# A two-layer decoder trunk: the copies of the latent keys and values out of PSUM move from VectorE to ScalarE

## The chip, the core and the metric

The kernel runs on one core of a Trainium2 chip. The metric is the device time of one execution in microseconds (us), given as a median over runs. Besides it there is one profiled execution of the kernel, from which every row below is taken.

## The reference: what is computed

The model has two layers over 256 tokens of width 1024. In each layer one wide input projection feeds three causal attentions side by side: a block-sparse one (A, 8 heads), a latent one (B, 8 heads) and a differential one (C, 4 heads). Each is gated and projected back, the three results are merged by sigmoid gates, projected once more, and a gated embedding and a layer norm end the layer. The change lies in the latent attention, of which this is the core:

```python
cq = _rmsnorm(b_cq, gq)                  # 256 x 384
ckv = _rmsnorm(b_ckv, gkv)               # 256 x 256
qh = _split_heads(cq @ w_uq, MLA_HEADS)
q_b = concat([qh[..., :64], rope(qh[..., 64:])])
kvh = _split_heads(ckv @ w_ukv, MLA_HEADS)
k_b = concat([kvh[..., :64], broadcast(rope(b_kr))])   # keys: 64 + 32 per head
yb = mla_attention(q_b, k_b, kvh[..., 64:])            # values: 64 per head
```

The product `ckv @ w_ukv` gives the latent keys (64 of the 96 rows of every head's key) and the latent values.

## The kernel before, in words

**Precision and weights.** Every large product is made of three matmuls: each operand is split into a high part (rounded to the fast 32-bit format) and a low part (the rest), and high x high, high x low and low x high are summed in PSUM (`mm3`, lines 236 to 239). Each piece of the weights is loaded on SP's queue into one of five raw buffers (line 167), cast to its high part on ScalarE (line 173) and subtracted to its low part on VectorE (line 174). There are three buffers for split pieces, so a cast can wait for TensorE to be done with an older piece; a raw buffer is free for the next load when the subtraction has read it.

**PSUM.** The eight banks form two pools of four. `ps_w` serves the projections in rotation: a projection takes the bank that the fourth one before it used, and has to wait until that one has been copied out. `ps_t` serves transposes, scores and attention outputs.

**Order of the work.** TensorE's order is written by hand: a list of projections ("fill") with the attention steps put in by due times (lines 923 to 984). The order of the other engines comes from a scheduler, engine by engine, each executing its queue in order. Around the change TensorE runs, in each layer: a gate projection (`gate`, bank name `pg`), transposes of attention A's probabilities (`tr_p`, bank name `tp`), the latent keys in two groups of four heads (`up_kn`, bank name `pn`), the latent values for two blocks of 128 tokens (`up_v`, bank name `pk`), again transposes, then the next gate projection (weights `hi_m`, `lo_m`), more of attention A, and the gate path of attention B (weights `hi_bz`, `lo_bz`, bank name `pa`). The four banks before that gate projection are thus the two `pn` and the two `pk`, and the gate projection takes over the bank of the first `pn`.

**Copies out of PSUM.** `nope` (lines 583 to 596) is used for the latent queries (tile `qb`) and keys (tile `kb`). Its bank holds 128 rows, two heads of 64 rows on top of each other; the upper half (`e == 0`) is copied by ScalarE (line 594), the lower half by VectorE (line 596). `up_v` copies its whole bank on VectorE (line 630) into tile `vb`. Keys are used by the scores of attention B (`sc`, lines 678 and 681), values some 50 us later (line 737).

Of the kernel before, what the change touches and what calls it, by code (L numbers as in the profile page):

```python
# [31 lines left out]
def tile_decoder_trunk(  # L32
# [24 lines left out]
    nc = tc.nc  # L57
# [25 lines left out]
    def bank(pool, name):  # L83
        return pool.tile([P, 512], F32, tag="bank", name=name)
# [143 lines left out]
    def W(key):  # L228
        i = state["use"]
        assert pieces[i][0] == key, (pieces[i][0], key)  # L230
        split_to(i + 1 + SPLIT_AHEAD)
        load_to(i + 1 + SPLIT_AHEAD + LOAD_AHEAD)
        state["use"] += 1
        return parts.pop(i)

    def mm3(o, lh, ll, rh, rl, start, stop):
        nc.tensor.matmul(o, lh, rh, start=start, stop=False)  # L237
        nc.tensor.matmul(o, lh, rl, start=False, stop=False)  # L238
        nc.tensor.matmul(o, ll, rh, start=False, stop=stop)  # L239
# [34 lines left out]
    NQ, NK = 3, 2  # L274
# [62 lines left out]
    def layer(li):  # L337
# [14 lines left out]
        T = {}  # L352
# [227 lines left out]
            nc.gpsimd.tensor_tensor(dst[:, :, 16:32], ta[:, :nh, 16:32], tb[:, :nh, 0:16],  # L580
                                    op=ALU.add)

        def nope(dst, w, act_t, nk, g2):
            o = bank(ps_w, "pn")
            for j in range(2):
                c0 = (2 * g2 + j) * P
                for k in range(nk):
                    mm3(o[:, j * S:(j + 1) * S], w[0][:, k, c0:c0 + P], w[1][:, k, c0:c0 + P],
                        act_t[:, 0, k, :], act_t[:, 1, k, :], k == 0, k == nk - 1)
            d = dst[0:64, 4 * g2:4 * g2 + 4, :].rearrange("p (j e) t -> p j e t", e=2)  # L590
            for e in range(2):
                src = o[64 * e:64 * e + 64, :].rearrange("p (j t) -> p j t", j=2)
                if e == 0:
                    nc.scalar.copy(d[:, :, e, :], src)
                else:
                    nc.vector.tensor_copy(d[:, :, e, :], src)  # L596

        def up_qn(g2):
            if g2 == 0:
                T["uqN"] = W(K("uqN"))  # L600
                T["qb"] = work.tile([P, 8, S], F32, tag="qk8", name=f"qb{li}")[:96]
            nope(T["qb"], T["uqN"], yc4, NQ, g2)
# [13 lines left out]
        def up_kn(g2):  # L616
            if g2 == 0:
                T["ukv"] = W(K("ukv"))
                T["kb"] = work.tile([P, 8, S], F32, tag="qk8", name=f"kb{li}")[:96]
            nope(T["kb"], [t[:, 0] for t in T["ukv"]], T["ckvT"], NK, g2)  # L620

        def up_v(b):
            if b == 0:
                T["vb"] = work.tile([P, 2, 512], F32, tag="v", name=f"vb{li}")
            wh, wl = [t[:, 1] for t in T["ukv"]]
            o = bank(ps_w, "pk")
            for k in range(NK):
                mm3(o, T["ckvT"][:, 0, k, b * P:(b + 1) * P], T["ckvT"][:, 1, k, b * P:(b + 1) * P],
                    wh[:, k, :], wl[:, k, :], k == 0, k == NK - 1)
            nc.vector.tensor_copy(T["vb"][:, b, :], o)  # L630

        def rope_k():
            for b in range(2):
# [297 lines left out]
        fill += [(2.13, up_qn, (0,)), (2.13, up_qn, (1,)), (1.06, up_qr, (0,)), (1.06, up_qr, (1,))]  # L931
        g_a(1)
        fill += [(1.42, up_kn, (0,)), (1.42, up_kn, (1,)), (1.4, up_v, (0,)), (1.4, up_v, (1,))]
        g_a(2)
        fill += [(H, bz, (g, j)) for g in range(2) for j in range(2)]
# [253 lines left out]
```

## Time and profile before

| | |
|---|---|
| median of 3 runs | 655.67 us (655.61 to 655.78) |
| the profiled execution, its own time | 656.14 us |
| its span in the trace | 654.4 us |
| ScalarE (ACT) busy | 368.5 us (56%), 729 instructions |
| GpSimd (POOL) busy | 109.8 us (17%) |
| granted TensorE clock, mean | 0.997 |

The span runs from the first to the last instruction of the trace; the execution's own time holds 1.7 us around it. Engines are PE (TensorE matmuls), PEld (its weight loads), DVE (VectorE), ACT (ScalarE), POOL (GpSimd) and SP (the DMA queue). Times in rows are microseconds from the span's start; L596 is line 596 of the kernel. A matmul's busy time reaches to its modelled end, so neighbours overlap: in a stream without waits a 256-column matmul starts every 0.12 us though each is shown with 0.28 us.

### The profile page before, as it was taken

How to read it: one execution, taken by the hardware profiler on the slowest of the kernel's cores; microseconds unless marked ns; L12 is line 12 of the kernel's file. 1: busy time of each engine (PE TensorE's matmuls, PEld its weight loads, DVE VectorE, ACT ScalarE, POOL GpSimd, SP SyncE). 2: the span in 40 equal slices, each digit the busy share in tenths (PEclk: the TensorE clock that was granted, in tenths of full speed). 3: DMA queues.
4: the chain of work that ended last, by engine and by line, in shares of the span. 5: the costliest groups of instructions: out<-in, count | busy, mean ns of one | idle time of the engine just before them, and what ended most of it. 6: DMA issues, size and time to landing. Idle time of an engine off the chain costs nothing.

```text
span 654.4 us, 11980 instructions
## 1 busy us (share of the span) xinstructions
PE 638.8 (98%) x4623; PEld 595.2 (91%) x4623; DVE 464.2 (71%) x884; ACT 368.5 (56%) x729; POOL 109.8 (17%) x139
## 2 busy tenths in 40 slices
PE   9999998999999999999999999989999999999994
PEld 6999988999989999988879999989998899999884
DVE  5658798786787566655895587987867866566566
ACT  5457685555675545544455576755656655444451
POOL 2060452010003220000020605511100032200002
PEclk9999999999999999999999999999999999999998
DMA  8765177454546665665446652774445465766511
GB/s 284 239 223 154 58 238 245 124 158 133 158 145 210 195 186 171 191 194 187 127 117 192 196 158 74 230 247 124 138 130 173 149 198 159 204 182 185 169 33 64
DMA packets 82796, 110.31 MB, mean 169 GB/s; under 512 B 3962, under 2 KB 59700, under 8 KB 82740
## 3 DMA queue, kind: packets, MB, share of 16 engines
q1 hardware_dynamic: 80832, 106.25, 53.0%
q10 hardware_dynamic: 1908, 3.31, 1.6%
q8 instruction: 36, 0.59, 0.4%
q14 instruction: 20, 0.16, 0.1%
HBM read 108.49 MB, written 1.05 MB: 167 GB/s over the span
## 4 chain that ended last, share of the span: by engine, by line
PE 66%; issue 15%; DVE 10%; ACT 5%; DMA 2%; POOL 2%; POOLq 0%; DVEq 0%; ACTq 0%
PE pg L237 5%; PE pg L239 5%; PE pg L238 5%; PE pa L237 5%; PE pa L238 5%; PE pa L239 5%; PE pb L239 5%; PE pb L238 5%; PE pb L237 4%; PE pbr L237 3%; PE pbr L239 3%; PE pbr L238 3%; PE sc L681 2%; PE pv L737 2%; PE tp L724 1%
## 5 line engine op out<-in xcount | busy, mean ns | idle before, releaser
L237 PE MATMUL pg<-act,hi_m 128*128 128x256 f32 x384 | 109.5, 285 | 4.6 <-DVE kb L596 3.4
L239 PE MATMUL pg<-act,lo_m 128*128 128x256 f32 x384 | 107.9, 281 | 0.0
L238 PE MATMUL pg<-act,hi_m 128*128 128x256 f32 x384 | 107.9, 281 | 0.0
L174 DVE TENSOR_TENSOR lo_m<-raw_m,hi_m 128x1024 fp32r<-128x1024 f32 x48 | 59.4, 1241 | 25.5 <-ACT hi_m L173 25.5
L237 PEld LDWEIGHTS pg<-act,hi_m 128*128 128x128 f32 x384 | 72.4, 188 | 5.3 <-DVE kb L596 3.9
L173 ACT CAST hi_m<-raw_m 128x1024 fp32r<-128x1024 f32 x48 | 49.7, 1053 | 43.4 <-PE pg L238 29.0
L238 PEld LDWEIGHTS pg<-act,hi_m 128*128 128x128 f32 x384 | 72.4, 189 | 0.1
L239 PEld LDWEIGHTS pg<-act,lo_m 128*128 128x128 f32 x384 | 72.4, 188 | 0.0
L237 PE MATMUL pbr<-act,hi_b 128*128 128x256 f32 x128 | 37.4, 292 | 0.0
L239 PE MATMUL pbr<-act,lo_b 128*128 128x256 f32 x128 | 36.0, 281 | 0.0
L238 PE MATMUL pbr<-act,hi_b 128*128 128x256 f32 x128 | 35.9, 281 | 0.0
L174 DVE TENSOR_TENSOR lo_b<-raw_b,hi_b 128x1024 fp32r<-128x1024 f32 x24 | 32.8, 1379 | 1.2 <-ACT hi_b L173 1.2
L173 ACT CAST hi_b<-raw_b 128x1024 fp32r<-128x1024 f32 x24 | 24.6, 1050 | 14.8 <-PE pbr L238 6.1
L1057 POOL TENSOR_TENSOR bnmv<-bnmv,mhalf 128x1 f32<-128x1 f32 x4 | 3.1, 780 | 164.4 <-DVE bnmv L1056 164.4
L174 DVE TENSOR_TENSOR lo_wo<-raw_wo,hi_wo 128x1024 fp32r<-128x1024 f32 x16 | 19.3, 1223 | 15.7 <-ACT hi_wo L173 15.7
L907 POOL TENSOR_TENSOR gz<-gz,subt 128x512 f32<-128x512 f32 x4 | 9.2, 2310 | 111.3 <-DVE sm1('c', 3)_6089 L695 53.7
L174 DVE TENSOR_TENSOR lo_pg<-raw_pg,hi_pg 128x1024 fp32r<-128x1024 f32 x16 | 19.2, 1221 | 9.4 <-ACT hi_pg L173 9.4
L173 ACT CAST hi_pg<-raw_pg 128x1024 fp32r<-128x1024 f32 x16 | 16.4, 1049 | 16.6 <-issue 7.2
L237 PE MATMUL pb<-hi_wo,act 128*128 128x512 f32 x64 | 25.5, 398 | 0.0
L238 PE MATMUL pb<-lo_wo,act 128*128 128x512 f32 x64 | 25.3, 395 | 0.0
L239 PE MATMUL pb<-hi_wo,act 128*128 128x512 f32 x64 | 25.3, 395 | 0.0
L173 ACT CAST hi_wo<-raw_wo 128x1024 fp32r<-128x1024 f32 x16 | 16.3, 1048 | 15.1 <-issue 12.1
(900 smaller groups left out, 2209.8 us busy)
## 6 DMA issues: line engine op xcount, KB each, us to landing
raw_m<-in_w_merge_dram SPq DMA_DIRECT2D x48, 512.0 KB, 3.7
raw_wo<-in_w_out_dram SPq DMA_DIRECT2D x16, 512.0 KB, 4.6
raw_pg<-in_w_ple_gate_dram SPq DMA_DIRECT2D x16, 512.0 KB, 4.4
raw_aq<-in_w_in_dram SPq DMA_DIRECT2D x8, 512.0 KB, 4.6
raw_ak<-in_w_in_dram SPq DMA_DIRECT2D x8, 512.0 KB, 5.5
raw_az<-in_w_in_dram SPq DMA_DIRECT2D x8, 512.0 KB, 5.8
raw_bz<-in_w_in_dram SPq DMA_DIRECT2D x8, 512.0 KB, 4.9
raw_b<-in_w_branch_a_dram SPq DMA_DIRECT2D x8, 512.0 KB, 4.7
```

Of the source, the lines that this page charges most:

```text
L173: nc.scalar.copy(h, r)
L174: nc.vector.tensor_sub(l, r, h.bitcast(F32))
L237: nc.tensor.matmul(o, lh, rh, start=start, stop=False)
L238: nc.tensor.matmul(o, lh, rl, start=False, stop=False)
L239: nc.tensor.matmul(o, ll, rh, start=False, stop=stop)
L681: nc.tensor.matmul(o[:, P:384], ql[:, P:S], kr[:, 0:S], start=first, stop=final)
L724: nc.tensor.transpose(t[:, k * P:(k + 1) * P], E[:, e, k * P:(k + 1) * P], ident)
L737: nc.tensor.matmul(o[64 * e:64 * e + 64, t0:t1], v[:, kb_, h * 64:(h + 1) * 64], pt[:, e, a0:a0 + t1 - t0], start=kb_ == 0, stop=kb_ == 1)
L907: nc.gpsimd.tensor_tensor(g4, g4, subt[:, li:li + 1, :].to_broadcast([P, 4, P]), op=ALU.mult)
L1057: nc.gpsimd.tensor_tensor(mv[:, b, 2:3], mv[:, b, 1:2], mhalf[:, 0:1], op=ALU.pow)
```

## The change

The copies of the latent keys and values out of PSUM are all made by ScalarE. `nope` gets a switch; with it, the lower half goes to ScalarE as well. The latent keys set it, the latent queries don't. The copy of the latent values changes from a VectorE to a ScalarE instruction.

```diff
-        def nope(dst, w, act_t, nk, g2):
+        def nope(dst, w, act_t, nk, g2, on_act=False):
...
-                if e == 0:
+                if e == 0 or on_act:
                     nc.scalar.copy(d[:, :, e, :], src)
                 else:
                     nc.vector.tensor_copy(d[:, :, e, :], src)
...
-            nope(T["kb"], [t[:, 0] for t in T["ukv"]], T["ckvT"], NK, g2)
+            nope(T["kb"], [t[:, 0] for t in T["ukv"]], T["ckvT"], NK, g2, True)
...
-            nc.vector.tensor_copy(T["vb"][:, b, :], o)
+            nc.scalar.copy(T["vb"][:, b, :], o)
```

On ScalarE, in the first layer, around the copies of the keys (`pt0('a', 2)` is a copy of transposed probabilities of attention A, `hi_bz` the casts of the next weights; minus is before, plus is now):

```order
 L726 COPY pt0('a', 1)_1290<-tp 128x384
 L173 CAST hi_bz_1370<-raw_bz_1237 128x1024
-L594 COPY kb_1311<-pn 64x2x256 x2
+L594 COPY kb_1311<-pn 64x2x256 x4
+L630 COPY vb_1342<-pk 128x512 x2
+L726 COPY pt0('a', 2)_1359<-tp 128x384
 L173 CAST hi_bz_1475<-raw_bz_1307 128x1024
-L726 COPY pt0('a', 2)_1359<-tp 128x384
 L173 CAST hi_bz_1475<-raw_bz_1309 128x1024
```

Two copies of keys become four, two copies of values follow, and the copy of the probabilities now stands ahead of both casts of the second `hi_bz` piece instead of between them.

On VectorE at the same place (`lo_bz` are the subtractions for the same weights):

```order
 L174 TENSOR_TENSOR lo_bz_1371<-raw_bz_1235,hi_bz_1370 128x1024
 L174 TENSOR_TENSOR lo_bz_1371<-raw_bz_1237,hi_bz_1370 128x1024
-L596 COPY kb_1311<-pn 64x2x256 x2
-L630 COPY vb_1342<-pk 128x512 x2
 L728 COPY pt0('a', 2)_1359<-tp 128x384
 L174 TENSOR_TENSOR lo_bz_1476<-raw_bz_1307,hi_bz_1475 128x1024
```

Four copies are gone there, and nothing else has moved. The second layer shows the same two pieces. TensorE's, GpSimd's and SP's instructions are the same in both kernels; on TensorE what they wait for changes at the gate projection after the keys and values (names with _49 are the engines' semaphores):

```order
 L724 MATMUL tp<-ident,E0('a', 2)_975 128x128 [waits Pool_49]
 L724 MATMUL tp<-ident,E0('a', 2)_975 128x128
-L237 MATMUL pg<-act_127,hi_m_1301 128x256 [waits DVE_49]
+L237 MATMUL pg<-act_127,hi_m_1301 128x256 [waits PE_49,Activation_49]
+L238 MATMUL pg<-act_127,hi_m_1301 128x256
+L239 MATMUL pg<-act_127,lo_m_1302 128x256 [waits DVE_49]
```

Its first matmul waited for VectorE; now it waits for ScalarE, and the third one for VectorE (for the low part of the weights).

## Rows read from the trace of the kernel before

**Rows 1.** Table of the page: busy us (share of the span), instructions, by engine.

```profile
PE 638.8 (98%) x4623; PEld 595.2 (91%) x4623; DVE 464.2 (71%) x884; ACT 368.5 (56%) x729; POOL 109.8 (17%) x139
```

**Rows 2.** Waits of TensorE: who waited for whom, us in total, times, longest.

```profile
PE pg L237 <- DVE kb L596: 3.4, 2, 1.7
PE pg L237 <- DVE qb L596: 1.2, 1, 1.2
```

**Rows 3.** Timeline of PE, first layer: start, us, instruction [idle before <-releaser].

```profile
93.13 0.82 PE L724 MATMUL tp<-ident,E0('a', 1)_911 128*128 128x128 f32 x6
93.71 0.36 PE L237 MATMUL pn<-ckvT,hi_ukv 128*128 128x256 f32 x1
...
99.41 0.82 PE L724 MATMUL tp<-ident,E0('a', 2)_975 128*128 128x128 f32 x6
101.94 0.39 PE L237 MATMUL pg<-act,hi_m 128*128 128x256 f32 x1 [1.71 <-DVE kb L596]
```

**Rows 4.** Timeline of PE, second layer, the same place.

```profile
425.18 0.82 PE L724 MATMUL tp<-ident,E1('a', 2)_4622 128*128 128x128 f32 x6
427.69 0.39 PE L237 MATMUL pg<-act,hi_m 128*128 128x256 f32 x1 [1.69 <-DVE kb L596]
```

**Rows 5.** Timeline of DVE, first layer, around the copies.

```profile
95.40 2.82 DVE L174 TENSOR_TENSOR lo_m<-raw_m,hi_m 128x1024 fp32r<-128x1024 f32 x2
...
98.61 2.55 DVE L174 TENSOR_TENSOR lo_bz<-raw_bz,hi_bz 128x1024 fp32r<-128x1024 f32 x2
101.19 1.30 DVE L596 COPY kb<-pn 64x512 f32<-64x512 f32 x2
102.52 1.29 DVE L630 COPY vb<-pk 128x512 f32<-128x512 f32 x2
...
104.19 2.35 DVE L174 TENSOR_TENSOR lo_bz<-raw_bz,hi_bz 128x1024 fp32r<-128x1024 f32 x2
```

**Rows 6.** Timeline of ACT, first layer, around the copies.

```profile
97.02 1.05 ACT L173 CAST hi_bz<-raw_bz 128x1024 fp32r<-128x1024 f32 x1 [1.61 <-DMA raw_bz<-in_w_in_dram]
97.98 1.06 ACT L594 COPY kb<-pn 64x512 f32<-64x512 f32 x2
99.61 1.05 ACT L173 CAST hi_bz<-raw_bz 128x1024 fp32r<-128x1024 f32 x1 [0.57 <-PE pk L239]
100.56 0.47 ACT L726 COPY pt0('a', 2)_1359<-tp 128x384 f32<-128x384 f32 x1
101.91 1.05 ACT L173 CAST hi_bz<-raw_bz 128x1024 fp32r<-128x1024 f32 x1 [0.88 <-DMA raw_bz<-in_w_in_dram]
107.80 1.05 ACT L173 CAST hi_m<-raw_m 128x1024 fp32r<-128x1024 f32 x1 [4.83 <-PE pg L238]
```

**Rows 7.** Timeline of ACT, second layer: the two key copies.

```profile
423.79 1.06 ACT L594 COPY kb<-pn 64x512 f32<-64x512 f32 x2
```

**Rows 8.** Instructions that write the keys: ns min/median/max, first and last start.

```profile
L594 ACT COPY kb<-pn x4: 575/581/584, 98.0 to 424.3; 64x512 f32<-64x512 f32 x4
L596 DVE COPY kb<-pn x4: 685/690/694, 101.2 to 427.6; 64x512 f32<-64x512 f32 x4
```

**Rows 9.** Instructions that use bank `pa`, 110 to 130 us: ScalarE's whole-bank read.

```profile
L532 ACT ACTIVATE tz<-pa x2: 589/594/599, 117.5 to 124.3; 128x512 f32<-128x512 f32 x2
```

**Rows 10.** The two loads of the next gate weights, issued 98.3 and 99.9 us.

```profile
L167 SPq DMA_DIRECT2D raw_m<-in_w_merge_dram x2: 368/368/368, 98.3 to 99.9; - x2
...
DMA to landing us min/median/max: 4.7/4.9/5.0
```

**Rows 11.** Waits of all engines: the longest of ScalarE's.

```profile
ACT hi_m L173 <- PE pg L238: 29.0, 8, 4.8
```

**Rows 12.** Busy time in stretches: PE, PEld, DVE, ACT, POOL (instructions), clock, DMA share, GB/s.

```profile
120.00:140.00 20.00, 20.00 (x168) 19.17 (x167) 15.55 (x46) 12.21 (x35) 2.83 (x3) 1.00 0.58 158
...
300.00:320.00 20.00, 20.00 (x94) 16.25 (x93) 15.17 (x20) 10.69 (x15) 0.00 (x0) 1.00 0.54 160
```

**Rows 13.** Timeline of PE: where the second `bz` piece is first used.

```profile
117.40 0.47 PE L237 MATMUL pa<-act,hi_bz 128*128 128x256 f32 x1
```

## The prediction

> **What bounds the kernel now.** I read the table of engines first. TensorE is busy for 638.8 of 654.4 us, and VectorE for 464.2 [rows 1]; so nothing but TensorE's own stream, and the few places where it stands still, can set the end. The second view is therefore the list of TensorE's waits. The longest entry by far is the one that this change touches: the gate projection's first matmul waited twice for VectorE's copy of the keys, 3.4 us in all [rows 2]. The reader is to see there that the next entry is far smaller, and that it, the wait for the copy of the queries (1.2 us), belongs to a part of `nope` that stays as it is.
>
> The third view is TensorE's timeline at these two places. In the first layer six transposes start at 99.41 and the gate projection at 101.94, with 1.71 us idle put down to `kb` on line 596 [rows 3]; in the second layer 425.18 and 427.69, idle 1.69 [rows 4]. The fourth view says why VectorE was late. Its queue held two subtractions for the weights `lo_bz`, 98.61 to 101.16; only at 101.19 did it come to the two copies of the keys [rows 5]. The products were there long before: ScalarE copied its halves of the same two banks from 97.98 to 99.04 [rows 6]. So the bank was half free at about 98.56 and wholly free only when VectorE's first copy ended, 101.19 + 0.69 = 101.88 [rows 5, 8]; 0.06 us later TensorE started. The wait is one for a place in VectorE's queue, not for the copy's duration.
>
> **The change, part by part.**
>
> *Removed from VectorE:* per layer two key copies of 0.69 us [rows 8] and two value copies that take 1.29 us together [rows 5], so about 2.6 us; over two layers 5.2. VectorE is not the bound, so this time by itself is worth nothing; what counts is the release of the bank.
>
> *Added to ScalarE:* per layer two key copies and two value copies. ScalarE's copy of such a half takes 0.58 us [rows 8], and two in a row take 1.06 [rows 6], so each further one adds 0.48. The whole-bank value copy on ScalarE does not occur in this trace. Its nearest row is ScalarE's pass over a whole bank of the same 128x512 shape, 0.594 us alone [rows 9]; the bounds are 0.48 (a key copy in a row) and 1.05 (a cast of twice as many elements [rows 6]). I take 0.50 in a row, next to the nearest row.
>
> *When the bank comes free.* The four key copies now stand together behind the cast that began at 97.02. The first two of them empty the first bank (its two halves), so it is free at 97.98 + 1.06 = 99.04; in the second layer 423.79 + 1.06 = 424.85 [rows 7]. TensorE wants it when its six transposes have been issued. How long that takes without a wait is shown a little earlier: transposes at 93.13, the next projection at 93.71, 0.58 us later [rows 3]. So it wants the bank at 99.41 + 0.58 = 99.99, and at 425.18 + 0.58 = 425.76. The bank is free 0.95 and 0.91 us before: the wait goes wholly. The weights that the projection also needs are there too, their low part since 95.40 + 2.82 = 98.22 [rows 5].
>
> *What that is worth.* 101.94 - 99.99 = 1.95 us in the first layer, 427.69 - 425.76 = 1.93 in the second; sum 3.88. The idle times of the timeline, 1.71 and 1.69 [rows 3, 4], give 3.40 and are the lower bound, since they count from the modelled end of the last transpose and not from the moment at which the next matmul could have started. I take 3.88, because the 0.58 is a start-to-start time of the same sequence.
>
> *What is late next on TensorE.* Nothing near. From 120 to 320 us TensorE is shown busy all the time: 20.00 of 20.00 us in the first and in the last of the stretches of 20 us between (ten in all) [rows 12]. What runs ahead of TensorE there hangs on TensorE: the casts of the gate weights waited 29.0 us for it in eight places [rows 11], the first of them just behind the change, 4.83 us before 107.80 [rows 6]. When TensorE comes 1.95 us earlier, that cast starts at 105.85 instead of 107.80, if its data are there; the loads were issued at 98.3 and 99.9 and landed 4.7 to 5.0 us later, the last by 104.9 [rows 10], 0.95 us before. All the following weights, their loads and subtractions then move with it.
>
> *What ScalarE delays.* Behind the key copies (last end 97.98 + 1.06 + 0.96 = 100.00) come two value copies (to 101.0), the copy of the probabilities (0.47 alone, to 101.4) and the two casts of `hi_bz` that began at 99.61 and 101.91. They now run from about 101.4 to 103.4. The first is later by 1.8 us. VectorE needs it for `lo_bz`, which started at 104.19 because of its copies [rows 5]; now it can start when the first cast is done, about 102.4, and ends by 104.8, where before it ended at 104.19 + 2.35 = 106.54. So the weights of the second `bz` piece are ready earlier in spite of the longer queue, and TensorE uses them only at 117.40 [rows 13], now 115.45: more than 10 us of cover. The raw buffers of these weights, and with them SP's next loads, come free earlier too. If that cover were gone, each us of ScalarE's delay would cost one.
>
> *The TensorE clock* is granted at 1.00, its higher level of 2.4 GHz, in the stretches after the change [rows 12]; I count no change there.
>
> **A rule that speaks against it.** Before, both engines emptied the banks of the keys, and the first bank was out at 101.88, when VectorE's half was done; two copies in a row on ScalarE end at 99.04 [rows 5, 6, 8]. The Trainium skill, TensorEngine Tiling (Array Packing), section PSUM Bottleneck, says to use both ScalarE and VectorE to empty PSUM. By that rule one engine alone frees the banks later and the change costs time, which is rival B below with its price and chance. The trace does not bear the rule out at this place: in a row on one engine the halves are out 2.84 us earlier than side by side on two, because one of the two had other work ahead.
>
> **The rivals.**
>
> *A. The gain is given back (no change).* Some later supply that doesn't depend on TensorE, a load or a chain on VectorE, could let TensorE wait 1.9 us further on. For it: VectorE is busy for 15.55 of 20 us in the next stretch [rows 12]. Against it: the casts wait for TensorE and not the reverse [rows 11], and the loads there have 0.95 us in hand [rows 10]. Time: 655.67, or 655.67 - 1.94 = 653.7 if only one layer gives it back.
>
> *B. ScalarE becomes the late engine (slower).* Its queue runs in order, and four more copies stand in it. The place: the cast of the gate weights, at 107.80 before, and behind it in the queue all that attention A and B get from ScalarE. The price: the added 0.96 + 1.0 = 1.96 us per layer. It decides from the point at which this exceeds ScalarE's idle time ahead of that cast: 4.83 us, less the 1.95 by which TensorE arrives earlier, is 2.88, to which 0.57 and 0.88 of earlier idle time come [rows 6]. If the whole addition stood on the path in both layers and the gap stayed, the time would be 655.67 + 3.92 = 659.6. Against it speaks that 1.96 is well under 2.88 even without the earlier gaps. The Trainium skill, PSUM — Partial Sum Buffer, section Engine vs sequencer instructions, says that ScalarE's queue is strictly first in, first out. The trace agrees, as the key copies stood idle until the cast ahead of them had its data at 97.02.
>
> *C. Partial: the load ahead is late.* The cast in front of the key copies waits for its load, 1.61 us before 97.02 [rows 6]. TensorE is ready 0.95 us after the bank is free, so a load later by more than that eats into the gain one to one; the kernel before would suffer from it as well. A load later by 2 us in both layers would leave 3.88 - 2 x 1.05 = 1.8: 653.9.
>
> That the change doesn't do what it says can be left out: the order of the instructions shows the copies on ScalarE, and TensorE's, GpSimd's and SP's unchanged.
>
> **How the numbers follow.** The profiled execution took 656.14 us, with 1.7 around its span, so the sum gives 656.14 - 3.88 = 652.26 there; it lay 0.47 above the median, and against the median the forecast is 655.67 - 3.88 = 651.79, rounded to 651.8. Chances: forecast 0.85; C or one layer alone 0.06; A 0.06; B 0.03. The forecast's own range is 655.67 - 3.95 to 655.67 - 3.40, so 651.7 to 652.3, with 0.3 on either side for runs: 651.4 to 652.6. Towards C I widen it to 653.7; below, to 651.2, in case VectorE's free time removes some tenths elsewhere. 0.2% is 1.3 us, about what can be told from no change; C and a gain in one layer alone lie beyond it. So: faster 0.91, within 0.2% 0.06, slower 0.03.
>
> **What would show it.** Right: the row of TensorE waiting for `kb` is gone from its waits; the gate projection starts 0.58 us after the transposes, near 99.99 and near 423.8 (425.76 less the first layer's 1.95); ScalarE's four key copies run from 97.98 to about 100.0; `lo_bz` starts near 102.4; the cast of the gate weights still waits for TensorE, by about 2.5 us; the span is near 650.5; the wait for `qb`, 1.2 us, is still there. Wrong: a new wait of TensorE for ScalarE at the gate projection (then the copies take longer in series than 0.48 each, or the load was late), a TensorE wait for weights between 100 and 320 us (rival A), or ScalarE busy without a break up to the cast of the gate weights (rival B).

## The result, and the profile after

The changed kernel takes 652.2 us (median of 4 runs, 650.53 to 652.35) against 655.72 of the kernel before: ratio 0.9942, 95% interval 0.9929 to 0.9956. The medians lie 3.5 us apart, and the interval stands for 2.9 to 4.7 us; 651.8 was predicted, in a range of 651.2 to 653.7. The profiled execution took 652.14 us with a span of 650.4, 4.0 less than the span before.

TensorE's waits in the trace after, longest first (who waited for whom, us in total, times, longest), answer to [rows 2]:

```profile
PE warmup L254 <- DVE warm L248: 1.0, 1, 1.0
PE pg L237 <- DVE qb L596: 0.9, 1, 0.9
PE pb L239 <- DVE bnmv L1056: 0.5, 1, 0.5
```

The row for `kb`, 3.4 us, is gone, and no wait for ScalarE has come in its place. The wait for `qb`, ahead of the change, is still there, 0.9 us in place of 1.2. Two more rows differ by 0.2 to 0.3 us each, waits for the first weights (`lo_cq`, `hi_av`) in the first 26 us of the span. TensorE's timeline after, first and second layer, answers to [rows 3, 4]:

```profile
99.37 0.82 PE L724 MATMUL tp<-ident,E0('a', 2)_975 128*128 128x128 f32 x6
99.95 0.37 PE L237 MATMUL pg<-act,hi_m 128*128 128x256 f32 x1
...
423.16 0.82 PE L724 MATMUL tp<-ident,E1('a', 2)_4622 128*128 128x128 f32 x6
423.73 0.37 PE L237 MATMUL pg<-act,hi_m 128*128 128x256 f32 x1
```

The reader is to see that the gate projection now starts 0.58 and 0.57 us behind the transposes, with no idle time noted; before it was 2.53 and 2.51. ScalarE's timeline after, first layer, answers to [rows 6]:

```profile
97.01 1.05 ACT L173 CAST hi_bz<-raw_bz 128x1024 fp32r<-128x1024 f32 x1 [1.62 <-DMA raw_bz<-in_w_in_dram]
97.97 2.37 ACT L594 COPY kb<-pn 64x512 f32<-64x512 f32 x4
100.37 1.07 ACT L630 COPY vb<-pk 128x512 f32<-128x512 f32 x2
101.33 0.50 ACT L726 COPY pt0('a', 2)_1359<-tp 128x384 f32<-128x384 f32 x1
101.70 2.02 ACT L173 CAST hi_bz<-raw_bz 128x1024 fp32r<-128x1024 f32 x2
105.80 1.04 ACT L173 CAST hi_m<-raw_m 128x1024 fp32r<-128x1024 f32 x1 [2.08 <-PE pg L238]
```

The queue stands as the order showed it. The four key copies take 2.37 us, 0.35 more than I had summed; the two value copies 1.07, as summed. The cast of the gate weights still waits for TensorE, 2.08 us. VectorE's timeline after, first layer, answers to [rows 5]:

```profile
98.58 2.54 DVE L174 TENSOR_TENSOR lo_bz<-raw_bz,hi_bz 128x1024 fp32r<-128x1024 f32 x2
101.05 0.54 DVE L728 COPY pt0('a', 2)_1359<-tp 128x384 f32<-128x384 f32 x1
102.80 2.36 DVE L174 TENSOR_TENSOR lo_bz<-raw_bz,hi_bz 128x1024 fp32r<-128x1024 f32 x2 [1.21 <-ACT hi_bz L173]
```

VectorE now waits 1.21 us for ScalarE's cast ahead of the second `lo_bz` and is still done at 105.16, where before it was done at 106.54. TensorE first uses this piece at 115.40. The durations of the moved copies (ns min/median/max), from the views of tile `kb` and tile `vb`, answer to [rows 8] and give the one that the trace before did not have:

```profile
L594 ACT COPY kb<-pn x8: 571/584/587, 98.0 to 423.5; 64x512 f32<-64x512 f32 x8
```

```profile
L630 ACT COPY vb<-pk x4: 590/592/592, 100.4 to 424.6; 128x512 f32<-128x512 f32 x4
```

### The profile page after: what moved, and what is told of

It is laid out like the page before. It is cut to its first block, busy times and chain, and to the rows that moved or that the text cites. A ratio compares the mean times of both kernels' runs of the same rounds, so it can differ in the third digit from the quotient of the medians.

```text
span 650.4 us, 11982 instructions
## 1 busy us (share of the span) xinstructions
PE 638.1 (98%) x4623; PEld 595.0 (91%) x4623; DVE 459.1 (71%) x876; ACT 372.9 (57%) x737; POOL 109.8 (17%) x139
## 4 chain that ended last, share of the span: by engine, by line
PE 72%; issue 15%; DVE 6%; ACT 3%; POOL 2%; DMA 2%; POOLq 0%; DVEq 0%
PE pg L237 6%; PE pg L239 6%; PE pg L238 6%; PE pa L237 5%; PE pa L238 5%; PE pa L239 5%; PE pb L239 4%; PE pb L238 4%; PE pb L237 4%; PE pbr L237 3%; PE pbr L239 3%; PE pbr L238 3%; PE sc L681 2%; PE tp L724 2%; PE pv L737 2%
```

## Experiments

Runs of one kernel differ by up to 2.5 us (the kernel before: 654.21 to 656.73 over all its runs), more than half of the effect. The traces show where this comes from. At the place of the change, the same six transposes start at 99.41 us in the kernel before, at 97.94 in one experiment and at 99.88 in another, though nothing that TensorE waits for ahead of that place was changed in any of these three; the waits that differ up to there are those for the first weights and for `qb` (in the latest of the three 0.8 us for `hi_av`, 0.4 for `lo_cq` and 0.9 for `qb`, in the earliest none of these). From that place to the end the traces agree to about 0.1 us where they have the same waits. So beside the measured times I give a second number for each: the span less the start of those transposes in the first layer, "from the transposes to the end". It is 654.4 - 99.41 = 554.99 us for the kernel before and 650.4 - 99.37 = 551.03 for the changed kernel, 3.96 less.

### Keys alone, values alone

Only the keys move (e1; the value copy is VectorE's again):

```diff
-            nc.scalar.copy(T["vb"][:, b, :], o)
+            nc.vector.tensor_copy(T["vb"][:, b, :], o)
```

> Only the copies of the latent keys move to ScalarE; the values stay on VectorE. Theory (the release of the first pn bank is all that counts): the whole gain, 3.9 us less than the kernel before, the gate projection starts 0.58 us after the transposes in both layers. Rival (what counts is the time taken off VectorE): about half of it, 1.9 us, since half of the moved time stays on VectorE.

Measured: 651.13 us, ratio 0.9942 (0.9930 to 0.9955), the same ratio as with keys and values. TensorE's timeline in this run, first layer:

```profile
98.23 0.82 PE L724 MATMUL tp<-ident,E0('a', 2)_975 128*128 128x128 f32 x6
98.81 0.37 PE L237 MATMUL pg<-act,hi_m 128*128 128x256 f32 x1
```

From the transposes to the end: 649.2 - 98.23 = 550.97. The whole gain is in the keys.

Only the values move (e2; edit against the kernel before):

```diff
-            nc.vector.tensor_copy(T["vb"][:, b, :], o)
+            nc.scalar.copy(T["vb"][:, b, :], o)
```

> Only the copies of the latent values move to ScalarE; VectorE still copies the lower halves of the keys at the same place in its queue. Theory: no gain (0 within 0.3 us), TensorE still waits 1.7 us for kb in both layers. Rival (time taken off VectorE): about 1.9 us less than before.

Measured: 655.2 us, ratio 0.9997 (0.9988 to 1.0005). TensorE's longest wait in this run, and its timeline:

```profile
PE pg L237 <- DVE kb L596: 3.4, 2, 1.7
```

```profile
97.94 0.82 PE L724 MATMUL tp<-ident,E0('a', 2)_975 128*128 128x128 f32 x6
100.46 0.39 PE L237 MATMUL pg<-act,hi_m 128*128 128x256 f32 x1 [1.70 <-DVE kb L596]
```

From the transposes to the end: 652.8 - 97.94 = 554.86, 0.13 less than before. VectorE has lost 1.3 us of work per layer here, and it is worth nothing. The rival that counts the time taken off VectorE falls with these two runs.

### The first key bank alone (e5)

```diff
-            nope(T["kb"], [t[:, 0] for t in T["ukv"]], T["ckvT"], NK, g2, True)
+            nope(T["kb"], [t[:, 0] for t in T["ukv"]], T["ckvT"], NK, g2, g2 == 0)
...
-            nc.scalar.copy(T["vb"][:, b, :], o)
+            nc.vector.tensor_copy(T["vb"][:, b, :], o)
```

> Only the lower half of the first key bank moves to ScalarE (one copy per layer); the second bank's and the values stay on VectorE. Theory (the first bank's release is the whole effect): 3.9 us less than the kernel before, as with all eight copies. Rival (each moved copy has its share): about a quarter of it, 1.0 us.

Measured: 652.98 us, ratio 0.9959 (0.9947 to 0.9971), 1.9 to 3.5 us less than before: below the 3.9 expected, and far above the rival's 1.0. The timelines of TensorE and of VectorE in this run:

```profile
99.88 0.82 PE L724 MATMUL tp<-ident,E0('a', 2)_975 128*128 128x128 f32 x6
100.45 0.37 PE L237 MATMUL pg<-act,hi_m 128*128 128x256 f32 x1
```

```profile
101.63 0.69 DVE L596 COPY kb<-pn 64x512 f32<-64x512 f32 x1
```

The gate projection does not wait, although VectorE copies the second key bank only at 101.63, after the projection has begun. So one copy per layer, that of the first bank's lower half, removes the wait for `kb`. What is missing stands in this run's list of waits:

```profile
PE pg L237 <- DVE qb L596: 1.3, 2, 0.9
```

TensorE waits for `qb` in both layers here, 0.9 and 0.4 us; the other traces have at most one such wait, in the first layer. The second layer's, in TensorE's timeline:

```profile
411.04 0.82 PE L724 MATMUL tp<-ident,E1('a', 0)_4486 128*128 128x128 f32 x6
412.29 0.39 PE L237 MATMUL pg<-act,hi_m 128*128 128x256 f32 x1 [0.43 <-DVE qb L596]
```

From the transposes to the end: 651.5 - 99.88 = 551.62, 0.59 above the changed kernel, and the added wait is about that size: the projection starts 1.25 us behind the six transposes, where in the changed kernel it is 0.57 (410.55 and 411.12), so 0.68 us late. VectorE copies `qb` there at 411.54, 1.20 us later than in the changed kernel, while TensorE is 0.49 us later; nothing of what VectorE does between the first layer's copies and this place was edited, and why it fell behind is not settled.

### VectorE's queue shortened, the copies left on VectorE (e3)

Against the kernel before, GpSimd makes one subtraction of the first `bz` piece (second half), which stood ahead of the key copies:

```diff
-                    split_op(hv[:, k0:k0 + nh, :], lv[:, k0:k0 + nh, :], rt)
+                    if key[:3] == "bz0" and k0:
+                        nc.scalar.copy(hv[:, k0:k0 + nh, :], rt)
+                        nc.gpsimd.tensor_sub(lv[:, k0:k0 + nh, :], rt,
+                                             hv[:, k0:k0 + nh, :].bitcast(F32))
+                    else:
+                        split_op(hv[:, k0:k0 + nh, :], lv[:, k0:k0 + nh, :], rt)
```

> All key and value copies stay where they were before the change; GpSimd instead of VectorE makes the second subtraction of the first bz piece, so that VectorE comes to the key copies about 1.2 to 1.4 us earlier. Theory (place in the queue, not the engine): VectorE's first key copy starts near 99.8 and ends near 100.5, TensorE starts right behind it, 1.4 us earlier per layer, 2.9 us in all, less what the slower subtraction on GpSimd costs where bz is used. Rival (ScalarE's faster copy is what helps): no gain.

Measured: 652.69 us, ratio 0.9963 (0.9951 to 0.9975). VectorE's, GpSimd's and TensorE's timelines in this run (line numbers are 5 higher):

```profile
97.80 1.21 DVE L174 TENSOR_TENSOR lo_bz<-raw_bz,hi_bz 128x1024 fp32r<-128x1024 f32 x1
99.04 1.30 DVE L601 COPY kb<-pn 64x512 f32<-64x512 f32 x2
```

```profile
100.39 2.40 POOL L226 TENSOR_TENSOR lo_bz<-raw_bz,hi_bz 128x1024 fp32r<-128x1024 f32 x1
```

```profile
98.59 0.82 PE L729 MATMUL tp<-ident,E0('a', 2)_975 128*128 128x128 f32 x6
99.79 0.38 PE L242 MATMUL pg<-act,hi_m 128*128 128x256 f32 x1 [0.38 <-DVE kb L601]
```

The key copies are on VectorE as before, and the projection starts 1.20 us after the transposes in place of 2.53. From the transposes to the end: 650.5 - 98.59 = 551.91, 3.08 less than before (2.9 expected). That the two numbers lie so close is in part luck: 0.4 of the 3.08 us lie behind TensorE's last matmul, which starts here and in the kernel before at

```profile
642.32 0.28 PE L244 MATMUL pgh<-hi_pg,act 128*128 128x256 f32 x1
```

```profile
645.79 0.28 PE L239 MATMUL pgh<-hi_pg,act 128*128 128x256 f32 x1
```

The span ends 8.2 us after it here, and 8.6 after it in the kernel before and in the changed one. From the transposes to the last matmul it is 543.73 us against 546.38, so 2.65 less, about twice the 1.33 by which the projection came earlier; in the changed kernel it is 542.42, 3.96 less. So two thirds of the gain come from the place in the queue, with no copy moved to ScalarE. The rest is missing because one subtraction still stands ahead: the first key copy ends at 99.04 + 0.69 = 99.73, where TensorE could have gone on at 98.59 + 0.58 = 99.17.

### How much room the copies on ScalarE have

Against the changed kernel, the copy of the first key bank's upper half is made two times (e6), and in a second kernel four times (e7):

```diff
-                    nc.scalar.copy(d[:, :, e, :], src)
+                    for _ in range(2 if on_act and g2 == 0 and e == 0 else 1):
+                        nc.scalar.copy(d[:, :, e, :], src)
```

(The second kernel has 4 in place of 2.)

> As the changed kernel, but ScalarE makes the copy of the first key bank's upper half twice (same data). It puts 0.5 to 0.6 us more ahead of the release of that bank, about 99.7 where TensorE wants it at 99.95. Theory (a margin of 0.8 to 0.95 us covers it): the same time as the changed kernel, 3.5 to 4 us less than before, no idle time ahead of the gate projection. Rival (TensorE stands right behind ScalarE's copies and every addition shows): 0.5 to 0.6 us per layer more than the changed kernel, 1.1 in all.

Measured: 652.07 us, ratio 0.9948 (0.9934 to 0.9962). ScalarE's and TensorE's timelines (line numbers are 1 higher in these two kernels):

```profile
97.86 2.98 ACT L595 COPY kb<-pn 64x512 f32<-64x512 f32 x5
```

```profile
99.24 0.82 PE L725 MATMUL tp<-ident,E0('a', 2)_975 128*128 128x128 f32 x6
99.81 0.37 PE L237 MATMUL pg<-act,hi_m 128*128 128x256 f32 x1
```

One more copy, 0.61 us, does not show at all: from the transposes to the end 650.2 - 99.24 = 550.96.

> As the changed kernel, but ScalarE makes that copy four times in place of once. It puts 1.5 to 1.8 us ahead of the release of the first key bank, beyond the margin. Theory: the gate projection waits for ScalarE by 0.65 to 1.0 us per layer, the time is 1.3 to 2.0 us above the changed kernel, 1.9 to 2.6 us below the kernel before. Rival (the order on ScalarE doesn't matter to TensorE as long as VectorE is relieved): no more time than the changed kernel.

Measured: 653.23 us, ratio 0.9968 (0.9955 to 0.9980). ScalarE's timeline, TensorE's, and TensorE's longest wait:

```profile
97.32 3.96 ACT L595 COPY kb<-pn 64x512 f32<-64x512 f32 x7
```

```profile
98.69 0.82 PE L725 MATMUL tp<-ident,E0('a', 2)_975 128*128 128x128 f32 x6
100.13 0.39 PE L237 MATMUL pg<-act,hi_m 128*128 128x256 f32 x1 [0.62 <-ACT kb L595]
```

```profile
PE pg L237 <- ACT kb L595: 1.2, 2, 0.6
```

The three more copies add 3.96 - 2.37 = 1.59 us, and the projection starts 1.44 us after the transposes, 0.86 late; so about 0.7 us of the 1.59 were covered. From the transposes to the end: 651.4 - 98.69 = 552.71, 1.68 above the changed kernel (1.3 to 2.0 expected). With this the margin is measured from both sides, between 0.61 and about 0.73 us. It also shows that nothing else on ScalarE is within these 1.6 us: the seven copies push back its casts, and behind the place of the change the only new wait of TensorE is the one for the bank.

### The queries as well

All latent queries move too (e4; edit against the changed kernel):

```diff
-            nope(T["qb"], T["uqN"], yc4, NQ, g2)
+            nope(T["qb"], T["uqN"], yc4, NQ, g2, True)
```

> As the changed kernel, and the lower halves of the latent queries on ScalarE as well. Theory (the same mechanism at the earlier gate projection): the wait for qb, 0.9 to 1.2 us in the first layer, goes; 0.9 to 1.2 us less than the changed kernel, about 5 us less than the kernel before. Rival (ScalarE's casts of the ukv weights, pushed back by 0.6 to 1.2 us, become late for the key projection): no gain over the changed kernel, a new wait of TensorE for hi_ukv or lo_ukv.

Measured: 650.73 us, ratio 0.9930 (0.9917 to 0.9944). The wait for `qb` is gone, and another one stands in the list:

```profile
PE pn L239 <- DVE lo_ukv L174: 0.6, 1, 0.6
```

So both theory and rival are half right. The rival's reason is not what the trace shows: ScalarE's first cast of these weights starts later (90.02, in the changed kernel 88.82), but VectorE comes to the subtraction only at 91.37, directly behind its other work. TensorE reaches the key projection 1.15 us earlier than in the changed kernel (92.53 and 93.68), VectorE the subtraction only 0.26 earlier (91.37 and 91.63). Both waits lie ahead of the transposes; from there to the end it is 650.1 - 99.12 = 550.98, as in the changed kernel. The other version (e8), keys whole, of the queries the first bank alone, values on VectorE:

```diff
-            nope(T["qb"], T["uqN"], yc4, NQ, g2)
+            nope(T["qb"], T["uqN"], yc4, NQ, g2, g2 == 0)
...
-            nc.scalar.copy(T["vb"][:, b, :], o)
+            nc.vector.tensor_copy(T["vb"][:, b, :], o)
```

> Keys wholly on ScalarE, values on VectorE, and of the latent queries the lower half of the first bank on ScalarE. Theory: the waits for kb in both layers go, and the wait for qb in the first layer (0 to 1.2 us, as the start of the layer falls) too; 4.0 to 5.0 us less than the kernel before, the fastest of all or level with the one that moves all queries. Rival (ScalarE's later casts of the ukv weights give it back): a new wait of TensorE for lo_ukv of about 0.6 us, level with keys alone.

Measured: 651.59 us, ratio 0.9949 (0.9936 to 0.9963), with a wait for `lo_ukv` of 0.2 us: not the fastest. To compare the three on one chip they were run again side by side (e9 to e11), without any edit.

> The changed kernel once more, on one chip with the next two, for a comparison among them. Theory: 3.9 us less than the kernel before, within what its first 100 us vary from run to run.

Measured: 652.16 us, ratio 0.9950 (0.9937 to 0.9964); from the transposes to the end 650.5 - 99.41 = 551.09.

> All copies of queries, keys and values on ScalarE, once more. Theory: the wait for qb in the first layer is gone (0 to 1.1 us), a wait for lo_ukv of 0.4 to 0.8 us stands in its place in some runs: 0 to 0.8 us less than the changed kernel. Rival (a real gain of its own): a full 1.1 us less.

Measured: 651.42 us, ratio 0.9940 (0.9926 to 0.9954). Neither `qb` nor `lo_ukv` is waited for in this trace.

> Keys and the first bank of the queries on ScalarE, values on VectorE, once more. Theory: 0.3 to 0.9 us less than the changed kernel, since its wait for lo_ukv is shorter (0.4 us) than where all queries move. Rival: level with the changed kernel within 0.3 us.

Measured: 652.72 us, ratio 0.9954 (0.9941 to 0.9966). Its trace has the wait for `lo_ukv` longest of all:

```profile
PE pn L239 <- DVE lo_ukv L174: 1.2, 2, 1.0
```

It was expected to be the shortest. VectorE still makes the second query copy in this version, at 90.07 us, ahead of the subtractions for `ukv`, and these come to 92.13; with all queries on ScalarE they began at 90.45 in e10, without a wait, and at 91.37 in e4, with one. So the same kernel has the wait in one trace and not in another, and what decides it is not settled. The version with all queries has the lowest median of the three, by 0.7 us against the changed kernel side by side; the intervals overlap (0.9926 to 0.9954 and 0.9937 to 0.9964), and whether it is faster stays open. Both versions are faster than the kernel before.

## Why the prediction was right, point by point

- *TensorE's stream and its waits set the end.* Right. The wait for `kb` went and the span fell by the sum of the two starts that moved (from 2.53 to 0.58 and from 2.51 to 0.57 behind the transposes, 3.89 in all, of a span shorter by 4.0); e2 shows the other side, 1.3 us less work on VectorE per layer with no change of the time.
- *The bank is late because of VectorE's queue.* Right, and shown by e3, where the copy stays on VectorE, only its queue is shorter by one subtraction, and TensorE gains 2.65 of the 3.96 us; and by e5, where one copy per layer is enough to remove the wait.
- *The sum.* 1.95 + 1.93 = 3.88 predicted. From the transposes to the end the traces differ by 3.96. The lower bound from the idle times, 3.40, was too low, as argued: the natural distance of 0.58 between transposes and projection came out as 0.58 and 0.57.
- *The copies in a row on ScalarE.* The one term that was mis-sized. I took 0.48 for each further key copy, from two upper halves in a row, though the trace before had no row of a lower half on ScalarE; four took 2.37 in place of 2.02, so 0.60 for each further one. The first bank was free at about 99.15, and its margin 0.8 us rather than 0.95; e6 shows that 0.61 us more are covered, e7 that of 1.59 about 0.7 are, since TensorE starts some 0.06 behind the end of the copy. It did not matter, since the margin was larger than the error. The value copy, for which the trace before had only a neighbour, was 0.592 alone and 0.48 in a row (0.594 and 0.50 taken).
- *What ScalarE delays.* `lo_bz` started at 102.80 (102.4 predicted), because of those 0.35 us, and ended 1.4 us earlier than before. The first use of the piece came at 115.40 (115.45).
- *What is late next.* Nothing came. The cast of the gate weights waited 2.08 us for TensorE (2.5 predicted).
- *Rival A* would have left a new wait of TensorE between 100 and 320 us; there is none. *Rival B* asked for ScalarE late at the cast of the gate weights; 2.08 us of idle time are left there, and even with three copies more the loss was only at the bank. *Rival C*, a late load ahead of the copies: the loads of the traces let the cast start with the same wait, 1.62 after and 1.61 before, so it did not arise, and it was not tested.
- *The rule on both engines.* The Trainium skill, TensorEngine Tiling (Array Packing), section PSUM Bottleneck, would have had the copies shared. The runs don't bear it out here: shared, the bank came at 101.88; on ScalarE alone at about 99.15; and shared again in e3 with a shorter queue the projection started at 1.20 us after the transposes, between the two.
- *The range.* It held the median; a single run lay outside below (650.53), within what the first layer's beginning varies. I had set aside 0.3 us for runs, and runs of one kernel differ by up to 2.5, so that the median of four lies within 0.4 us of the forecast is in part luck. The 3.95 at the larger end of the forecast's gain has no working: the sum is 3.88.

## What to carry to other kernels

When TensorE waits for a PSUM bank, look at what stands ahead of the copy in its engine's queue before looking at the copy: here a copy of 0.69 us cost TensorE 1.9 us because two subtractions came first; moving the copy won all of it, and moving one of the subtractions two thirds. Only the copy that frees the next bank counted; moving the values' was worth nothing. The Trainium skill, Perfetto Trace Analysis, section Optimizing Scalar/DVE Operations, says that moving some work to ScalarE may make sense where VectorE is saturated; here VectorE was busy 71% of the span, and what decided was the order within some 3 us, not its load.

## What the runs showed that was not expected

- ScalarE's copies of the two halves of a bank did not overlap: in a row they start 0.58 to 0.61 us apart, each taking 0.58, so four take 2.37 us; two copies of the upper halves in the kernel before take 1.06 together [rows 6] and two of whole banks 1.07 after, 0.48 apart. The halves differ in that the lower one is written to other partitions than it is read from; that this is the cause was not tested. In e7 two of the steps between the seven copies are 0.48 and the other four 0.59 to 0.61; the trace does not tell which half each of them reads.
- GpSimd's subtraction of 128x1024 took 2.40 us in e3, where VectorE's takes 1.21; VectorE's two subtractions in that stretch took 2.97 us in place of 2.35, while GpSimd was at work for part of it (VectorE 102.04 to 105.01, GpSimd 100.39 to 102.79). It is the first of the two, the one that overlaps GpSimd's, that is longer: 1.83 us in the first layer and 1.84 in the second. That GpSimd's work makes it so was not tested by itself.
- The beginning of the first layer varies by up to 1.9 us from run to run (97.94 to 99.88 at the same instruction), and the part after it by about 0.1 us between traces with the same waits, except for the last 8 us of e3.
